# One scan per four state-space groups, with a coefficient tile that holds zeros, in place of four scans

## The chip, the core and the metric

The kernel runs on one core of one Trainium2 chip. The metric is the device time of one execution in microseconds (us), the median of several runs. TensorE (PE) multiplies matrices and loads its weights in parallel (PEld), VectorE (DVE), ScalarE (ACT) and GpSimd (POOL) work on tiles elementwise, and SyncE (SP), ACT and POOL issue DMAs. Each engine takes its instructions strictly in program order and waits at the first one whose inputs are not ready.

## The reference

One decoder layer over 512 tokens of width 1024. What matters here is the middle of it, the mixer:

```python
h = h + 0.5 * swiglu(rmsnorm(h), ...)             # first feed-forward half
z = rmsnorm(h) @ w_in                             # q, three k/v pairs, gates, u
o_nsa = nsa_attention(q, ..., gates)              # compressed, selected and windowed attention
o_s5  = s5_mixer(u, ...)                          # 32 groups of 16 channels, 64 complex states each
h = h + concat([o_nsa, o_s5]) @ w_out
h = h + 0.5 * swiglu(rmsnorm(h), ...)             # second feed-forward half, then a gated embedding
# s5_mixer, per group: x[t] = a * x[t-1] + b u[t],  y[t] = Re(c x[t]) + d u[t]
```

## The kernel before, in words

The feed-forward halves take the time from 0 to about 370 us and from about 650 us to the end; the mixer lies between. The activations are held transposed, weights come in units of 128x1024 through ACT's DMA queue, and each unit is split into two parts, `hi` (ACT, line 164) and `lo` (DVE, line 166), so that three matmuls with those parts give one product close to float32.

The state-space part ("S5") handles 512 tokens as 64 chunks of 8 tokens. `s5_in(j)` runs for j = 0 to 7, each for GC = 4 of the 32 groups: four small matmuls give `w` in the PSUM bank `ps_C`, four DVE operations turn it by a rotation that makes the decay real (`t1`, lines 982 to 985), a scan along the 64 chunks follows with one real coefficient per partition and group (`r8`), and one operation turns the result back into `z`. `s5_out(j)` multiplies `z`, the input `u8` and the constants `so` into the bank `ps_D`; ACT copies the outcome into `ysb` (line 1012) and then makes the constants `so` for the next j by two copies (`swapped`, line 998). After every second j, `s5_back` transposes `ysb` back into `yt`.

Around it the mixer does the projections (24 matmuls into `ps_A` each) and their rotary turn: `rotary` forms `r` and `rb` from two projections and the tables in `turn`, and sends the outcome through DRAM by SP's queue: `kd` for the keys, which come back as `kf` and are cast into `KA` (ACT) and `KB` (DVE); `qd` for the queries, which come back as `qf` and are cast into `QA` and `QB` (ACT lines 1261 and 1262, DVE line 1263). The compressed keys take the way `ra`, `kcd`, `cst`, `cs`, and the compressed values `ra`, `vcd`, `cst`, and then the space of `turn`. The score groups of a query block (three matmuls: `KA`, `KB` and the mask, into `ps_B` or `ps_C`, two buffers each) are followed by a row maximum on DVE (`nmax`, line 1284) and an exponential on ACT (line 916) that frees the buffer.

The order of the mixer's steps is given by a table of step names (`PLAN`). That is the order in which the program is written; the order on each engine is then made by a scheduler, which lets an instruction pass others when it expects, from its own estimate of durations, that its inputs are ready sooner. So another duration at one place changes the order of others around it. The two feed-forward halves and all steps from the values of query block 2 on have the same order in both kernels.

Of the kernel before, what the change touches and what calls it, by code (L numbers as in the profile page):

```python
# [10 lines left out]
F32 = mybir.dt.float32  # L11
# [4 lines left out]
OP = mybir.AluOpType  # L16
# [14 lines left out]
GC = 4  # L31
# [45 lines left out]
def block_kernel(ctx: ExitStack, tc: tile.TileContext, a: dict, out: bass.AP):  # L77
    nc = tc.nc
    V, S, G, PE = nc.vector, nc.scalar, nc.gpsimd, nc.tensor
# [12 lines left out]
    def bank(tag, shape=(128, 512), dt=F32):  # L92
        return psum.tile(list(shape), dt, tag=tag, name="ps_" + tag)
# [38 lines left out]
    def mm(o, lhsT, rhs, start, stop, **kw):  # L132
        return PE.matmul(o, lhsT, rhs, start=start, stop=stop, **kw)  # L133
# [417 lines left out]
    r8 = pers.tile([128, NG], F32, name="r8")  # L551
# [295 lines left out]
    def mixer(ctx):  # L847
# [31 lines left out]
        s5w = s5x.enter_context(tc.tile_pool(name="s5w", bufs=2, reuse_waits="tile"))  # L879
# [88 lines left out]
        zs = [s5w.tile([128, 2, GC, 64], F32, name="z", bufs=1, tag=f"z{i}") for i in range(2)]  # L968
        for z in zs:
            G.memset(z[:, :, :, 0:1], 0.0)  # L970

        def s5_in(j):
            si_ = s5w.tile([128, GC, 256], F32, tag="si", name="si", bufs=3)
            G.dma_start(si_, s5i[:, GC * j:GC * j + GC])
            so = s5w.tile([128, GC, 384], F32, tag="so", name="so")
            G.dma_start(so[:, :, 0:256], s5o[:, GC * j:GC * j + GC])
            co, si = si_[:, :, 128:192], si_[:, :, 192:256]
            w = bank(TW, (128, GC, 64))
            for g in range(GC):
                mm(w[:, g], si_[:, g, 0:128], u8[:, GC * j + g], True, True)  # L980
            t1, t2 = (s5w.tile([128, GC, 64], F32, tag=n, name=n, bufs=1) for n in ("t1", "t2"))
            V.tensor_tensor(t1, w, co, OP.mult)
            V.tensor_tensor(t2[64:128], w[0:64], si[0:64], OP.mult)
            V.tensor_tensor(t2[0:64], w[64:128], si[64:128], OP.mult)
            V.tensor_tensor(t1, t1, t2, OP.subtract)
            vv = s5w.tile([128, GC, 64], F32, tag="vv", name="vv", bufs=1)
            for g in range(GC):
                V.tensor_tensor_scan(vv[:, g], r8[:, GC * j + g:GC * j + g + 1].to_broadcast([128, 64]), t1[:, g],  # L988
                                     0.0, OP.mult, OP.add)
            z = zs[j % 2]  # L990
            cs_ = si_.rearrange("p g (a c) -> p a g c", c=64)[:, 2:4, :, 0:63]
            V.tensor_tensor(z[:, :, :, 1:64], vv[:, None, :, 0:63].to_broadcast([128, 2, GC, 63]), cs_, OP.mult)
            return so, z
# [34 lines left out]
        def s5_all():  # L1028
            pend = s5_in(0)
            swapped(pend[0], nm.scaled)  # L1030
            yield
            for j in range(NCH):
                nxt = s5_in(j + 1) if j + 1 < NCH else None
                yield
                if j % 2 == 0:
                    ysb = s5w.tile([64, 8, 128], F32, tag="ysb", name="ysb", bufs=1)
                last = s5_out(j, ysb, *pend)
                if nxt:
                    swapped(nxt[0], last)
                if j % 2:  # L1040
                    s5_back(j // 2, ysb)
                pend = nxt
                yield
# [379 lines left out]
    with ExitStack() as mctx:  # L1423
        out_half = mixer(mctx)
# [357 lines left out]
```

## Time and profile before

| | |
|---|---|
| median of 3 runs | 1042.17 us (1041.87 to 1045.31) |
| the profiled execution | 1042.74 us, its span 1041.0 us |
| PE busy | 1027.3 us (99% of the span) |
| DVE busy | 823.0 us (79%) |
| ACT busy | 506.2 us (49%) |
| POOL busy | 161.4 us (16%) |

Times in the trace count from the start of the span. A row of the timeline gives start and duration in us, the engine, the line of the program, the operation, output and inputs, the shape, how many instructions were merged, and in brackets how long the engine sat idle before it and what released it. Matmuls overlap: their listed durations are longer than the distance from one start to the next, so the distance of starts tells the pace.

### The profile page before, as it was taken

To read this page: it belongs to the slowest core of one execution; us is meant where nothing else is said; L and a number is where in the kernel's file an instruction comes from. 1 tells how busy PE (TensorE), PEld (TensorE's weight loads), DVE (VectorE), ACT (ScalarE), POOL (GpSimd) and SP (SyncE) were. 2 spreads that over 40 slices of the span, in tenths; PEclk is the share of its full clock that TensorE was granted. 3 is DMA by queue.
4 is the path that set the end of the run, shared out by engine and by line. 5 is a ranking of instruction groups with operands and counts; after the bars stand their busy time and mean duration, and the time that the engine had idled before them with its cause. 6 is when DMAs were issued, how large, how long until landed. Compare 5 with 4: busy or idle time off the path is not lost.

```text
span 1041.0 us, 15686 instructions
## 1 busy us (share of the span) xinstructions
PE 1027.3 (99%) x6048; PEld 875.4 (84%) x6049; DVE 823.0 (79%) x1382; ACT 506.2 (49%) x872; POOL 161.4 (16%) x181
## 2 busy tenths in 40 slices
PE   9999999999999999999999999999999999999997
PEld 6888888889989888777586688998999899899886
DVE  6799468988989766996789887996598588687676
ACT  6322232535326542667768855663365245255452
POOL 0003948207870200100000000000000000000001
PEclk9999999999999999999999999999999999999999
DMA  7424325736344739566510023433323333333412
GB/s 253 157 84 134 101 82 165 240 122 128 122 129 149 234 113 225 174 208 177 167 41 21 21 69 128 128 103 121 95 91 119 101 102 101 101 103 104 146 54 82
DMA packets 50618, 129.98 MB, mean 125 GB/s; under 512 B 10608, under 2 KB 17424, under 8 KB 50544
## 3 DMA queue, kind: packets, MB, share of 16 engines
q10 hardware_dynamic: 26352, 90.77, 27.7%
q0 software_dynamic: 6592, 18.48, 6.9%
q1 hardware_dynamic: 17600, 19.73, 6.2%
q8 instruction: 47, 0.77, 0.3%
q14 instruction: 27, 0.22, 0.1%
HBM read 112.81 MB, written 15.73 MB: 123 GB/s over the span
## 4 chain that ended last, share of the span: by engine, by line
PE 85%; DVE 6%; POOL 3%; issue 2%; DMA 2%; ACT 2%; SPq 0%; DVEq 0%; ACTq 0%; POOLq 0%
PE ps_A L133 25%; PE ps_C L133 25%; PE ps_B L133 20%; PE ps_D L133 15%; POOL ft L721 1%; POOL bt L720 1%; DVE lo L166 1%; DMA raw<-in_wpack 1%; DMA kd<-r 1%; DVE vv L988 0%; DMA h<-in_xT 0%; POOL ft L719 0%; DVE s L342 0%; POOL seen L559 0%; PE ps_D L727 0%
## 5 line engine op out<-in xcount | busy, mean ns | idle before, releaser
L164 ACT CAST hi<-raw 128x1024 fp32r<-128x1024 f32 (+2 forms) x143 | 144.4, 1010 | 248.9 <-PE ps_C L133 97.2
L133 PE MATMUL ps_C<-hq,hi 128*128 128x512 f32 x704 | 217.4, 390 | 0.2
L166 DVE TENSOR_TENSOR lo<-raw,hi 128x1024 fp32r<-128x1024 f32 (+2 forms) x143 | 173.4, 1213 | 42.9 <-ACT hi L164 42.1
L133 PEld LDWEIGHTS ps_C<-hq,hi 128*128 128x128 f32 x704 | 130.8, 188 | 28.0 <-DVE h L526 1.3
L133 PE MATMUL ps_C<-hq,lo 128*128 128x512 f32 x352 | 136.9, 389 | 0.0
L133 PE MATMUL ps_A<-xh,hi 128*128 128x512 f32 (+1 forms) x352 | 124.2, 353 | 0.4 <-ACT hi L164 0.4
L133 PE MATMUL ps_A<-xl,hi 128*128 128x512 f32 (+1 forms) x352 | 124.1, 352 | 0.3 <-DVE xl L192 0.3
L133 PE MATMUL ps_A<-xh,lo 128*128 128x512 f32 (+1 forms) x352 | 122.6, 352 | 0.5 <-DVE lo L166 0.5
L164 ACT CAST hi<-s 128x1024 fp32r<-128x1024 f32 x56 | 59.0, 1053 | 107.0 <-PE ps_D L133 63.6
L166 DVE TENSOR_TENSOR lo<-s,hi 128x1024 fp32r<-128x1024 f32 x56 | 70.6, 1262 | 20.2 <-ACT hi L164 20.0
L133 PEld LDWEIGHTS ps_C<-hq,lo 128*128 128x128 f32 x352 | 66.1, 188 | 13.9
L133 PEld LDWEIGHTS ps_A<-xh,hi 128*128 128x128 f32 x352 | 66.4, 189 | 10.5 <-ACT hi L164 0.7
L133 PEld LDWEIGHTS ps_A<-xh,lo 128*128 128x128 f32 x352 | 66.5, 189 | 9.8 <-DVE lo L166 1.1
L133 PEld LDWEIGHTS ps_A<-xl,hi 128*128 128x128 f32 x352 | 66.5, 189 | 9.8 <-DVE xl L192 0.8
L526 DVE SCALAR_TENSOR_TENSOR h<-ps_C,h 128x512 f32<-128x512 f32 x64 | 43.9, 686 | 36.6 <-PE ps_C L133 36.4
L133 PE MATMUL ps_B<-sh,lo 128*128 128x256 f32 x224 | 63.1, 282 | 0.3 <-DVE lo L166 0.3
L133 PE MATMUL ps_D<-sl,hi 128*128 128x256 f32 x224 | 63.1, 282 | 0.0
L133 PE MATMUL ps_B<-sh,hi 128*128 128x256 f32 x224 | 63.0, 281 | 0.0
L133 PE MATMUL ps_B<-sl,hi 128*128 128x256 f32 x224 | 62.9, 281 | 0.0
L133 PE MATMUL ps_D<-sh,hi 128*128 128x256 f32 x224 | 62.8, 280 | 0.0
L133 PE MATMUL ps_B<-xh,hi 128*128 128x512 f32 (+1 forms) x168 | 62.8, 374 | 0.0
L133 PE MATMUL ps_D<-sh,lo 128*128 128x256 f32 x224 | 62.6, 280 | 0.0
(435 smaller groups left out, 2473.2 us busy)
## 6 DMA issues: line engine op xcount, KB each, us to landing
raw<-in_wpack ACTq DMA_DIRECT2D x168, 512.0 KB, 3.6
si<-s5i POOLq DMA_DIRECT2D x8, 512.0 KB, 5.5
so<-s5o POOLq DMA_DIRECT2D x8, 512.0 KB, 5.7
h<-in_xT SPq DMA_DIRECT2D x8, 256.0 KB, 4.3
s5i<-fs POOLq DMA_DIRECT2D x1, 2048.0 KB, 11.4
xraw<-in_xT SPq DMA_DIRECT2D x8, 256.0 KB, 3.4
s5o<-gt POOLq DMA_DIRECT2D x1, 2048.0 KB, 13.3
s5i<-tcs POOLq DMA_DIRECT2D x2, 1024.0 KB, 10.5
```

What stands on the lines that cost most here:

```text
L133: return PE.matmul(o, lhsT, rhs, start=start, stop=stop, **kw)
L164: p, q = S.copy(hi[:, c], raw[:, c]), None
L166: q = V.tensor_tensor(lo[:, c], raw[:, c], hi[:, c].bitcast(F32), OP.subtract)
L526: V.scalar_tensor_tensor(h[:, m, :], o[m], 0.5, h[:, m, :], OP.mult, OP.add)
L720: G.tensor_tensor(bt, b2[:, 1], bc(psn[:, e]), OP.mult)
L721: G.tensor_tensor(ft[:, :, s_, :], ft[:, :, s_, :], bt, OP.add)
```

## The change

A tile `decay` (128 partitions, 4 groups, 64 chunks) gets a zero at the first chunk of each group once, by POOL. In each `s5_in(j)` ACT copies the four coefficients of each partition into the other 63 places of each group, and DVE runs one scan over all 256 places. The zero makes the state start anew at each group. The tile is single, so the copy for j waits for the scan of j-1, and the scan of j waits for the copy. The result `vv` now takes the space of `t2`; both are used by DVE alone.

```diff
+        decay = s5w.tile([128, GC, 64], F32, name="decay", bufs=1)
+        G.memset(decay[:, :, 0:1], 0.0)
...
-            vv = s5w.tile([128, GC, 64], F32, tag="vv", name="vv", bufs=1)
-            for g in range(GC):
-                V.tensor_tensor_scan(vv[:, g], r8[:, GC * j + g:GC * j + g + 1].to_broadcast([128, 64]), t1[:, g],
-                                     0.0, OP.mult, OP.add)
+            S.copy(decay[:, :, 1:64], r8[:, GC * j:GC * j + GC, None].to_broadcast([128, GC, 63]))
+            vv = s5w.tile([128, GC, 64], F32, tag="t2", name="vv", bufs=1)
+            V.tensor_tensor_scan(vv.rearrange("p g c -> p (g c)"), decay.rearrange("p g c -> p (g c)"),
+                                 t1.rearrange("p g c -> p (g c)"), 0.0, OP.mult, OP.add)
```

Lines behind the change stand two further down in the new kernel. The scheduler's order changes on every engine inside the mixer. Three places of it follow. A number behind a name tells buffers apart.

The first place is DVE at the first pair of query projections (`r_4033` and `rb_4034` before, `r_4031` and `rb_4032` now), while the keys are under way through DRAM. Before:

```order
L1055 TENSOR_TENSOR r_3935<-r_3935,rb_3936 128x512
L1056 TENSOR_TENSOR r_3937<-r_3937,r_3938 128x512
L166 TENSOR_TENSOR lo<-raw,hi 128x1024
L1051 TENSOR_TENSOR r_4033<-ps_A,turn 128x512
L1052 TENSOR_TENSOR r_4035<-ps_A,turn 128x512
L1053 TENSOR_TENSOR rb_4034<-ps_A,turn 128x512
L1054 TENSOR_TENSOR r_4036<-ps_A,turn 128x512
L1072 TENSOR_TENSOR KB<-kf,KA 64x512
```

All four products of the queries with the tables stood ahead of the first `KB`, which needs the keys back from DRAM. The same stretch of DVE in the new kernel:

```order
L1057 TENSOR_TENSOR r_3933<-r_3933,rb_3934 128x512
L166 TENSOR_TENSOR lo<-raw,hi 128x1024
L1058 TENSOR_TENSOR r_3935<-r_3935,r_3936 128x512
L1053 TENSOR_TENSOR r_4031<-ps_A,turn 128x512
L166 TENSOR_TENSOR lo<-raw,hi 128x1024
L1054 TENSOR_TENSOR r_4033<-ps_A,turn 128x512
L1074 TENSOR_TENSOR KB<-kf,KA 64x512
L1055 TENSOR_TENSOR rb_4032<-ps_A,turn 128x512
L1056 TENSOR_TENSOR r_4034<-ps_A,turn 128x512
```

Two of the four products now stand behind the first `KB`.

The second place is where the second pair of queries comes back from DRAM as `qf`. ACT before, from the split of a unit of 840 columns on:

```order
L164 CAST hi<-raw 128x840
L1023 COPY yt<-ps_D 128x512
L916 ACTIVATE gt<-yt 128x512
L1261 ACTIVATE QA<-qf 64x512
L1262 ACTIVATE QB<-qf 64x512
L1012 COPY ysb<-ps_D 64x2x8x16
L916 ACTIVATE ps_B,den<-ps_B,nmax 128x512
L1012 COPY ysb<-ps_D 64x2x8x16
L998 COPY so<-so 64x4x128 x2
```

Here the copies `yt` and `gt` were done while `qf` was awaited. ACT in the new kernel:

```order
L988 COPY decay<-r_121 128x4x63
L164 CAST hi<-raw 128x840
L1263 ACTIVATE QA<-qf 64x512
L1264 ACTIVATE QB<-qf 64x512
L1025 COPY yt<-ps_D 128x512
L916 ACTIVATE gt<-yt 128x512
L1014 COPY ysb<-ps_D 64x2x8x16 x2
L1000 COPY so<-so 64x4x128 x2
```

`yt` and `gt` moved behind the two casts that need `qf`, and ahead of `ysb` and `so`. DVE at the same place, before:

```order
L1284 TENSOR_REDUCE nmax<-ps_B 128x1
L166 TENSOR_TENSOR lo<-raw,hi 128x840
L1084 TENSOR_TENSOR ra<-ra,rb_4347 64x512
L1085 TENSOR_TENSOR ra<-ra,rb_4347 64x512
L922 SCALAR_TENSOR_TENSOR gt<-gt,yt 128x512
L1263 SCALAR_TENSOR_TENSOR QA<-qf,QA 64x512
```

The compressed keys `ra` were finished ahead of the operation that needs `qf`. DVE in the new kernel:

```order
L166 TENSOR_TENSOR lo<-raw,hi 128x840
L1286 TENSOR_REDUCE nmax<-ps_B 128x1
L1265 SCALAR_TENSOR_TENSOR QA<-qf,QA 64x512
L1086 TENSOR_TENSOR ra<-ra,rb_4337 64x512
L1087 TENSOR_TENSOR ra<-ra,rb_4337 64x512
L922 SCALAR_TENSOR_TENSOR gt<-gt,yt 128x512
```

The operation on `qf` moved ahead of both `ra`.

The third place is DVE where the compressed values come back (`cst`) and are put into the space of `turn`. Before:

```order
L1284 TENSOR_REDUCE nmax<-ps_C 128x1
L1263 SCALAR_TENSOR_TENSOR QA<-qf,QA 64x512
L1284 TENSOR_REDUCE nmax<-ps_B 128x1 x2
L1131 TENSOR_TENSOR turn<-cst,pe 128x8x32 x2
L922 SCALAR_TENSOR_TENSOR gt<-gt,yt 128x512
L1131 TENSOR_TENSOR turn<-cst,pe 128x8x32 x2
```

Two row maxima of `ps_B` stood ahead of all four. In the new kernel:

```order
L1286 TENSOR_REDUCE nmax<-ps_C 128x1
L1133 TENSOR_TENSOR turn<-cst,pe 128x8x32 x2
L1286 TENSOR_REDUCE nmax<-ps_B 128x1
L1133 TENSOR_TENSOR turn<-cst,pe 128x8x32 x2
L922 SCALAR_TENSOR_TENSOR gt<-gt,yt 128x512
L1286 TENSOR_REDUCE nmax<-ps_B 128x1
```

Both maxima moved behind operations on `cst`. On PE the groups of `s5_out` moved among the projections too: those of j = 2, 3 and 5 (counted from 0) come 4, 2 and 6 matmuls of `ps_A` earlier than before, and six more value matmuls (128x280) stand ahead of the eighth score group of `ps_B`.

## Prediction

> **What bounds the kernel now.** I read the head of the page first, then the busy times by stretches of the mixer.
>
> ```profile
> span 1041.0 us, 15686 instructions
> PE 1027.3 (99%) x6048; PEld 875.4 (84%) x6049; DVE 823.0 (79%) x1382; ACT 506.2 (49%) x872; POOL 161.4 (16%) x181
> ...
> 400.00:420.00 20.00, 20.00 (x110) 16.45 (x109) 13.66 (x28) 5.07 (x8) 1.90 (x3) 1.00 0.84 229
> 420.00:440.00 20.00, 20.00 (x156) 15.94 (x156) 19.60 (x43) 14.15 (x24) 2.63 (x4) 1.00 0.56 179
> 440.00:460.00 20.00, 19.92 (x146) 15.60 (x143) 19.38 (x40) 13.79 (x29) 2.81 (x4) 1.00 0.71 218
> 460.00:480.00 20.00, 18.17 (x145) 15.04 (x145) 16.37 (x33) 15.38 (x36) 1.41 (x2) 0.91 0.62 146
> 480.00:500.00 20.00, 20.00 (x132) 12.82 (x131) 10.33 (x21) 12.98 (x30) 0.57 (x1) 1.00 0.68 237
> ```
>
> The columns after the width are the busy times of PE, PEld, DVE, ACT and POOL, then the granted clock. PE is the bound over the whole span: its matmuls stay the same, so only its gaps can be won or made. The stretch that holds the scans (400 to 466 us) has DVE at 97 to 98% from 420 to 460 us, with PE still fed, and only one gap of note behind it. The timeline of PE shows that gap:
>
> ```profile
> 463.02 0.39 PE L133 MATMUL ps_A<-hi,xl 128*128 128x280 f32 x1
> 465.24 0.50 PE L133 MATMUL ps_B<-KA,QA 128*128 128x512 f32 x1 [1.83 <-ACT ps_B L916]
> ...
> 466.47 0.43 PE L133 MATMUL ps_A<-hi,xl 128*128 128x280 f32 x1
> 466.70 0.43 PE L133 MATMUL ps_A<-hi,xh 128*128 128x280 f32 x1
> ...
> 470.02 0.29 PE L133 MATMUL ps_A<-hi,xh 128*128 128x280 f32 x1
> 470.15 0.29 PE L133 MATMUL ps_A<-lo,xh 128*128 128x280 f32 x1
> ...
> 465.30:469.30 4.00, 4.00 (x16) 3.19 (x17) 3.91 (x7) 3.90 (x10) 0.00 (x0) 0.57 0.85 218
> ```
>
> PE sat idle 1.83 us before the eighth score group in `ps_B`. Right behind it, the granted clock in a stretch of 4.0 us was 0.57, and the matmuls of 280 columns start 0.23 us apart instead of 0.13. At half clock for about 3.4 us (0.43 x 4.0 / 0.5) that cost another 1.7 us. So gap and slow stretch together are worth 3.5 us. What ended last there:
>
> ```profile
> 441.65 0.68 DVE L1056 TENSOR_TENSOR r<-r,r 128x512 f32<-128x512 f32 x1
> ...
> 442.36 0.32 SPq L1058 DMA_DIRECT2D qd<-r  x1
> 448.09 0.59 SPq L1250 DMA_DIRECT2D qf<-qd  x1
> 451.21 1.19 SPq L1087 DMA_DIRECT2D kcd<-ra  x2
> ...
> 456.82 1.78 SPq L1250 DMA_DIRECT2D qf<-qd  x2
> ...
> 450.79 0.63 ACT L1261 ACTIVATE QA<-qf 64x512 fp32r<-64x512 f32 x1 [3.13 <-DMA qf<-qd]
> ...
> 453.54 1.25 ACT L998 COPY so<-so 64x512 f32<-64x512 f32 x2
> ...
> 463.24 0.63 ACT L1261 ACTIVATE QA<-qf 64x512 fp32r<-64x512 f32 x1 [3.57 <-DMA qf<-qd]
> ...
> 464.41 0.66 ACT L916 ACTIVATE ps_B<-ps_B,nmax 128x512 f32<-128x512 f32 x1
> ```
>
> The exponential at 464.41 us frees the buffer for the eighth score group. It stood on ACT behind two casts of `qf` that waited for a DMA until 463.24. That DMA was issued behind the way of the compressed keys (`kcd`, `cst`), and that way starts when DVE has made `ra`. So a chain of DVE order and DRAM round trips sets the gap, and not the length of the scans alone.
>
> **The change, part by part.** First the scan.
>
> ```profile
> L988 DVE TENSOR_TENSOR_SCAN vv<-r,t x32: 260/266/293, 401.3 to 463.0; 128x64 f32<-128x64 f32 x32
> ...
> 400.85 0.42 DVE L985 TENSOR_TENSOR t<-t,t 128x256 f32<-128x256 f32 x1
> 401.31 0.84 DVE L988 TENSOR_TENSOR_SCAN vv<-r,t 128x64 f32<-128x64 f32 x4
> 402.18 0.68 DVE L992 TENSOR_TENSOR z<-vv,si 128x504 f32<-128x504 f32 x1
> ...
> L1012 ACT COPY ysb<-ps_D x16: 349/369/372, 411.7 to 474.4; 64x256 f32<-64x256 f32 x16
> ...
> 427.84 0.63 ACT L1261 ACTIVATE QA<-qf 64x512 fp32r<-64x512 f32 x1 [0.18 <-DMA qf<-qd]
> ...
> 434.00 0.63 ACT L916 ACTIVATE gt<-gt 128x512 f32<-128x512 f32 x1 [2.61 <-DVE gt L922]
> ```
>
> One scan lists 0.266 us, but four occupy only 0.84, since they overlap (0.19 us apart). A single pass over 256 places is not in the trace. The elementwise rows give 0.26 us more for 248 more places, so 1.04 ns each and 0.15 us fixed; a scan of 64 is then 0.115 us over its fixed part, or 1.8 ns a place, and 256 places take 0.61 us. The bounds are 0.47 us (0.266 plus 192 places at 1.04 ns) and 0.84 us (four times the pitch, no gain). I take 0.61, from the scans' own row. DVE is relieved of 0.23 us in each of eight steps, 1.8 us in all (0 to 3.0). [...]
>
> ACT gains eight copies of 252 places, 0.37 us each by the row of `ysb`: 3.0 us on an engine that has 6 us to spare in each 20 from 420 to 460 us. The first stands where ACT waits anyway. The others add a wait on DVE: a copy waits for the scan before it, and all behind it on ACT wait too. At j = 3 the copy and the second `so` (0.37 and 0.62) stand ahead of the first `QA`, which before started at 427.84, so it and `QB`, `yt` and `gt` behind it start about 1.0 us later; ACT sat idle 2.61 us soon after, at 434.00, and DVE takes up `QA` only later. I cost that at nothing; if the cover goes, it is that 1.0 us. The zeros cost POOL one memset, in front of loads needed 50 us later: nothing. `vv` in the space of `t2` adds no wait, as DVE runs both in order.
>
> Now the moved steps; here lies the rest of the sum. At the first place of the order DVE waits for the keys:
>
> ```profile
> 415.19 0.69 DVE L1051 TENSOR_TENSOR r<-ps_A,turn 128x512 f32<-128x512 f32 x1 [2.91 <-DMA kd<-r]
> ...
> 417.37 0.69 DVE L1053 TENSOR_TENSOR rb<-ps_A,turn 128x512 f32<-128x512 f32 x1 [0.89 <-PE ps_A L133]
> 417.98 0.68 DVE L1054 TENSOR_TENSOR r<-ps_A,turn 128x512 f32<-128x512 f32 x1
> ...
> 419.64 0.68 DVE L1072 TENSOR_TENSOR KB<-kf,KA 64x512 fp32r<-64x512 f32 x1 [0.98 <-ACT KA L1070]
> ```
>
> The products at 417.37 and 417.98 filled that wait. Behind `KB` they fall into the stretch where DVE is full: 1.2 us more work there (two starts 0.6 us apart). The `z` of j = 4 also moves ahead of the second query outcome, 0.6 us. Against that stand three scans (-0.7) and, by the shorter scans of j = 0 and 1, an earlier write of the keys (-0.3). So the outcome that before started at 441.65 comes 0.8 us later, and with it its write, the load of `qf` (its wait of 5.3 us from 442.7 to 448.09 is for that write) and ACT's `QA`: 451.6 us.
>
> The second place needs four rows more, two of ACT and two of PE:
>
> ```profile
> 446.41 0.59 ACT L1023 COPY yt<-ps_D 128x512 f32<-128x512 f32 x1
> 447.03 0.63 ACT L916 ACTIVATE gt<-yt 128x512 f32<-128x512 f32 x1
> ...
> 454.84 0.39 PE L133 MATMUL ps_A<-xh,lo 128*128 128x512 f32 x1
> 455.07 0.39 PE L133 MATMUL ps_A<-xh,hi 128*128 128x512 f32 x1
> 455.38 0.66 PE L133 MATMUL ps_D<-so,z 128*64 128x128 f32 x8
> ```
>
> `yt` and `gt` (0.59 + 0.63) now stand between `QB` and `ysb`. ACT then runs 451.6 + 1.25 (QA, QB) + 1.2 + 0.75 (`ysb`) + 1.25 (`so`) = 456.0. On PE, `s5_out(5)` waits for that `so`. It started at 455.38, 0.6 us after `so` was done (453.54 + 1.25), and now stands 6 matmuls earlier, 6 x 0.23 = 1.4 us, so PE arrives at 454.0 and finds `so` at 456.1: a new gap of 2.1 us. On DVE, the operation on `qf` now blocks `ra`: DVE goes on at 452.3 instead of having `ra` done at 451.2, so `kcd` leaves at 453.6, 2.4 us later. SP issues in order, so the `cst` loads, the second `qf`, and the exponential behind its casts move by 2.4 us too. The eighth score group starts at 465.24 + 2.4 = 467.65. Six more matmuls of 280 columns (0.77 us) are done before it, so the net loss is 1.6 us. Seen from PE's gaps: 2.1 new, the old one 1.35 instead of 1.83.
>
> At the third place the ninth and tenth maxima stand behind `cst` of the values, which comes at least 2.4 us later. Counted by the same rows, the exponential for the tenth group comes about 1.3 us after PE wants it. This is the least sure term; between 0 and 1.3 I take 0.8, since ACT's order there has exponentials of `ps_C` that may be ready or not. The slow stretch of 1.7 us I leave as it is: one before, one after. The rest of the mixer (to 600 us) has nearly no gaps to win, and its new order I cost at nothing.
>
> Sum: scan on PE's path 0, since the relief is spent inside the chain (it is in the 0.8), + 1.6 + 0.8 = +2.4 us. The profiled execution took 1042.74 us, 1.7 over its span and 0.6 over the median; the sum stands against it, and I apply the difference to the median: 1042.17 + 2.4 = 1044.6 us, 0.23% slower. About 0.3%, or 3.1 us, is what a measurement of this kernel can tell from no change.
>
> **Rivals.** *Both gaps turn into slow stretches.* The new gap of 2.1 us is longer than the one that was followed by half clock. If each is followed by one, 1.7 us come on top, and with the third place in full (1.3) the loss is 1.6 + 1.7 + 1.3 = 4.6 us: 1046.8. Against it: PE at half clock arrives later at the second gap and so shrinks it. [...]
>
> *The old gap closes: faster.* The price is 1.83 + 1.7 = 3.5 us, so 1038.7. Of the gap of 1.83 us, the six matmuls cover 0.77 anyway, so the chain would have to come 1.1 us earlier than before, not 2.4 later. The writes of the queries land like this (size, then the median us to landing):
>
> ```profile
> qd<-r SPq DMA_DIRECT2D x4, 256.0 KB, 2.4
> ```
>
> The second query write was slower here, with 5.3 us until `qf` could be issued; 2 us less would bring `QA` to 449.6, before DVE and ACT stand at it. For it: the DMA share is 0.71 there, and the order of transfers changes. Against it: the same transfers remain, and the write itself starts later.
>
> *The moves cancel.* The new gap at `s5_out(5)` is lost from the old one, and nothing is left at the third place: within 1 us of 1042.2. It holds if `kf` comes 1 us earlier than I think and the 0.8 falls away.
>
> **How the numbers follow.** My forecast (+2.4, between +1 and +4) has 0.42, the two slow stretches 0.24, the cancelling 0.20, and the closed gap 0.14. Faster by over 0.3% is most of the last case and none of the others: 0.12. Slower by over 0.3% is the second case, 0.24, and the upper third of the first, 0.14: 0.38. Within 0.3%: 0.50. The range reaches from the closed gap at half of its price (1042.2 - 1.8 = 1040.4) to the second case with the cover of the copies gone as well (1046.8 + 1.0 = 1047.8). The unknown price of the scan moves the chain by three steps of at most 0.23 us one way and 0.14 the other, 0.7 or 0.4 us, and lies within that.
>
> **What would show it.** Right: scans of 0.6 to 0.7 us in eight rows; DVE idle about 3.5 us before the first `KB` and about 2 us before `QA` near 450; a gap of PE before `ps_D<-so,z` near 454 and a shorter one before the eighth score group near 466; `kcd` near 453.6. Wrong: no gap at 454, `QA` near 449, or a granted clock of 1.00 in all stretches from 440 to 480; or gaps of PE beyond 500 us, where I expect none.

## The result and the profile after

| | before | after |
|---|---|---|
| median of 6 runs each | 1042.81 us (1041.64 to 1045.31) | 1049.41 us (1048.83 to 1051.53) |
| ratio | | 1.0069, 95% interval 1.0053 to 1.0086 |
| the profiled execution and its span | 1042.74 us, 1041.0 us | 1049.26 us, 1047.4 us |

The changed kernel is slower by 0.69%, about 7 us. I forecast 1044.6 us, with a range up to 1047.8. The head of the page and the busy times by stretch of the changed kernel (columns as in the prediction):

```profile
span 1047.4 us, 15676 instructions
PE 1028.8 (98%) x6048; PEld 876.1 (84%) x6049; DVE 822.2 (78%) x1358; ACT 508.9 (49%) x880; POOL 160.7 (15%) x182
...
420.00:440.00 20.00, 18.82 (x135) 14.73 (x133) 18.64 (x32) 14.32 (x25) 2.63 (x4) 1.00 0.50 157
440.00:460.00 20.00, 18.31 (x144) 14.28 (x145) 18.21 (x30) 12.78 (x27) 2.28 (x4) 1.00 0.64 207
460.00:480.00 20.00, 17.21 (x131) 13.96 (x129) 15.50 (x29) 13.11 (x29) 1.94 (x3) 0.91 0.59 159
480.00:500.00 20.00, 18.28 (x133) 12.89 (x133) 10.93 (x22) 14.27 (x34) 0.00 (x0) 1.00 0.65 184
```

From 420 to 500 us PE is busy for 72.6 of 80 us, before for 78.1: 5.5 of the 6.4 us by which the span grew. DVE is less busy from 420 to 480 us than before, not more: it waits too. PE's gaps in the timeline:

```profile
432.09 0.66 PE L133 MATMUL ps_D<-so,z 128*64 128x128 f32 x8 [0.54 <-DVE z L994]
439.99 0.66 PE L133 MATMUL ps_D<-so,z 128*64 128x128 f32 x8 [0.63 <-ACT so L1000]
443.50 0.50 PE L133 MATMUL ps_B<-KA,QA 128*128 128x512 f32 x1 [1.31 <-ACT ps_B L916]
457.71 0.66 PE L133 MATMUL ps_D<-so,z 128*64 128x128 f32 x8 [0.38 <-ACT so L1000]
470.68 0.50 PE L133 MATMUL ps_B<-KA,QA 128*128 128x512 f32 x1 [2.79 <-ACT ps_B L916]
480.46 0.36 PE L133 MATMUL ps_A<-hi,xh 128*128 128x280 f32 x1 [0.28 <-DVE gp L1115]
494.54 0.43 PE L133 MATMUL ps_A<-raw,cs 128*63 128x256 f32 x1 [1.43 <-DMA raw<-in_wpack]
```

Before there was one gap of 1.83 us in all this. Now there are seven, 7.4 us together. The changed operations themselves look harmless (duration in ns: least, median, most):

```profile
L990 DVE TENSOR_TENSOR_SCAN vv<-decay,t x8: 680/691/693, 401.6 to 467.7; 128x256 f32<-128x256 f32 x8
L988 ACT COPY decay<-r x8: 395/402/402, 344.5 to 460.8; 128x252 f32<-128x252 f32 x8
```

So the reader has to follow the chain of waits. On DVE, then on SP's queue, then on ACT:

```profile
420.28 0.68 DVE L1074 TENSOR_TENSOR KB<-kf,KA 64x512 fp32r<-64x512 f32 x1 [4.65 <-ACT KA L1072]
...
425.15 0.68 DVE L1058 TENSOR_TENSOR r<-r,r 128x512 f32<-128x512 f32 x1
...
433.27 0.68 DVE L1265 SCALAR_TENSOR_TENSOR QA<-qf,QA 64x512 fp32r<-64x512 f32 x1 [0.54 <-ACT QA L1263]
...
444.69 0.68 DVE L1058 TENSOR_TENSOR r<-r,r 128x512 f32<-128x512 f32 x1
...
454.00 0.69 DVE L1265 SCALAR_TENSOR_TENSOR QA<-qf,QA 64x512 fp32r<-64x512 f32 x1 [1.11 <-ACT QA L1263]
...
455.44 0.69 DVE L1087 TENSOR_TENSOR ra<-ra,rb 64x512 f32<-64x512 f32 x1
...
465.38 1.09 DVE L1133 TENSOR_TENSOR cs<-cst,pe 128x256 f32<-128x256 f32 x2 [2.69 <-DMA cst<-kcd]
...
469.08 0.68 DVE L1286 TENSOR_REDUCE nmax<-ps_B 128x1 f32<-128x512 f32 x1
```

```profile
429.55 0.62 SPq L1252 DMA_DIRECT2D qf<-qd  x1
...
450.69 0.58 SPq L1252 DMA_DIRECT2D qf<-qd  x1
455.44 1.20 SPq L1089 DMA_DIRECT2D kcd<-ra  x2
460.16 0.46 SPq L1125 DMA_DIRECT2D cst<-kcd  x1
```

```profile
432.61 0.63 ACT L1263 ACTIVATE QA<-qf 64x512 fp32r<-64x512 f32 x1 [2.53 <-DMA qf<-qd]
...
453.34 0.63 ACT L1263 ACTIVATE QA<-qf 64x512 fp32r<-64x512 f32 x1 [3.63 <-DMA qf<-qd]
...
469.85 0.66 ACT L916 ACTIVATE ps_B<-ps_B,nmax 128x512 f32<-128x512 f32 x1 [1.98 <-DVE nmax L1286]
```

Four rows of before that the prediction does not show:

```profile
422.16 0.69 DVE L1056 TENSOR_TENSOR r<-r,r 128x512 f32<-128x512 f32 x1
...
425.13 0.62 SPq L1250 DMA_DIRECT2D qf<-qd  x1
...
454.33 0.46 SPq L1123 DMA_DIRECT2D cst<-kcd  x1
...
459.33 1.12 DVE L1131 TENSOR_TENSOR cs<-cst,pe 128x256 f32<-128x256 f32 x2
```

Read against the rows of before: the first query outcome (`L1058`, then `L1056` at 422.16) comes 3.0 us later, its `qf` is loaded 4.4 us later (then 425.13), the first `QA` runs 4.8 us later (427.84), and DVE now waits for it. The second outcome is 3.0 us late (441.65), its `QA` 2.6 (450.79). Behind that `QA` stands `ra`, so `kcd` leaves 4.2 us late (451.21). Its write took 4.7 us until `cst` could be loaded, against 3.1 before (451.21 to 454.33), so `cst` is 5.8 us late, and `cs` on DVE 6.0 (459.33). The row maximum behind `cs` waits with it, then the exponential, and PE stands 2.79 us. So 3.0 us at the first outcome have become 6.0 at `cs`. About 0.3 us of each of these delays is older than all this: the first scan starts at 401.6 us, before at 401.3. The rest of the way has three steps that add to the delay. The first query write took longer (from the start of its second half at 425.86 to the load 3.7 us, before 2.25 from 422.88), `ra` stood behind the wait for `QA` (4.2 us late at `kcd` against 2.6 at `QA`), and the write of `kcd` took 1.6 us longer. Half clock follows that gap as before (the stretch behind it):

```profile
470.70:474.70 4.00, 4.00 (x17) 3.63 (x18) 3.47 (x6) 3.92 (x9) 0.00 (x0) 0.57 0.76 203
```

### The profile page after: what moved, and what is told of

It reads as the page before. It is cut to its first block, busy times and chain, and to the rows that moved or that the text cites. A ratio compares the mean times of both kernels' runs of the same rounds, so it can differ in the third digit from the quotient of the medians.

```text
span 1047.4 us, 15676 instructions
## 1 busy us (share of the span) xinstructions
PE 1028.8 (98%) x6048; PEld 876.1 (84%) x6049; DVE 822.2 (78%) x1358; ACT 508.9 (49%) x880; POOL 160.7 (15%) x182
## 4 chain that ended last, share of the span: by engine, by line
PE 83%; DVE 5%; DMA 4%; POOL 3%; ACT 3%; issue 2%; SPq 0%; DVEq 0%; ACTq 0%; POOLq 0%
PE ps_C L133 24%; PE ps_A L133 23%; PE ps_B L133 20%; PE ps_D L133 15%; POOL ft L721 1%; POOL bt L720 1%; DVE lo L166 1%; DMA qf<-qd 1%; DMA raw<-in_wpack 1%; DMA qd<-r 0%; DMA h<-in_xT 0%; DMA kd<-r 0%; DMA kf<-kd 0%; POOL ft L719 0%; DVE s L342 0%
```

## The experiments

To part the arithmetic from the order, the instructions of the mixer are tied, engine by engine, into a given order by edges that set the order of issue and add no wait:

```diff
+for engine, places in ORDER.items():          # places in the order of tracing
+    for a, b in zip(places, places[1:]):
+        tc.add_manual_dep(kept[engine][b], kept[engine][a].name, nosync, reason="order")
```

Below, the fences show which rows move. The kernel before ran beside each, and all ratios are to it; its median moved between 1041.57 and 1042.81 us, so compare the ratios of two rows rather than their times.

| kernel | median us (least to most, runs) | ratio, 95% interval |
|---|---|---|
| changed | 1049.41 (1048.83 to 1051.53, 6) | 1.0069 (1.0053 to 1.0086) |
| four scans, new order | 1049.47 (1048.95 to 1050.86, 6) | 1.0067 (1.0049 to 1.0085) |
| one scan, old order | 1044.35 (1039.68 to 1047.20, 12) | 1.0007 (0.9988 to 1.0025) |
| changed, first place as before | 1048.53 (1047.35 to 1049.78, 6) | 1.0055 (1.0038 to 1.0072) |
| changed, `ra` first | 1046.18 (1045.32 to 1047.99, 7) | 1.0039 (1.0025 to 1.0054) |
| changed, `ra` and maxima as before | 1045.52 (1044.48 to 1045.87, 5) | 1.0035 (1.0023 to 1.0047) |
| changed, second place as before | 1045.29 (1043.29 to 1048.38, 12) | 1.0027 (1.0014 to 1.0041) |
| changed, DVE as before to 458 us | 1043.81 (1042.49 to 1047.77, 12) | 1.0025 (1.0016 to 1.0034) |
| one scan, old order up to 460 us | 1043.27 (1041.50 to 1046.21, 12) | 1.0011 (0.9999 to 1.0023) |
| one scan, old order, maxima early | 1041.59 (1040.20 to 1044.48, 12) | 0.9995 (0.9984 to 1.0007) |
| four scans, old order, maxima early | 1040.62 (1039.56 to 1044.77, 12) | 0.9988 (0.9974 to 1.0002) |
| four scans, the same and `KB` behind | 1040.69 (1038.90 to 1042.32, 11) | 0.9982 (0.9968 to 0.9996) |
| one scan, the same and `KB` behind | 1040.23 (1038.86 to 1041.64, 12) | 0.9980 (0.9970 to 0.9990) |

### Order or arithmetic

One scan with the old order:

```diff
 ORDER = every engine's order of the kernel before
+the scan of j where the four scans of j stood
+each copy into decay where ACT sat idle before
```

> One scan and the eight copies as in the changed kernel, but every engine's order in the mixer tied to that of the kernel before (each scan where the four stood, each copy where ACT sat idle before). If the loss of 6.6 us comes from the order alone: 1042 us, between 1040.5 and 1043.5, with PE gaps as before (one of about 1.8 us before the eighth score group near 465 us, half clock behind it). If the copies and the longer single scan make the loss: 1048 to 1050, with gaps before the matmuls that need z.

Four scans with the new order:

```diff
 ORDER = every engine's order of the changed kernel
-S.copy(decay...), one scan
+the four scans of j where the one scan of j stood
```

> Four scans without copies, as in the kernel before, but every engine's order in the mixer tied to that of the changed kernel. If the order makes the loss: 1049 us, between 1047.5 and 1050.5, with gaps near 432, 440, 443.5 and 470 us. If the copies and the single scan make it: 1042 to 1043.

The first gives 1.0007, the second 1.0067: the loss goes with the order and not with the scan or the copies (the interval of the first leaves room for at most 2.6 us of theirs). The gaps of the second stand where the changed kernel's do:

```profile
443.25 0.50 PE L133 MATMUL ps_B<-KA,QA 128*128 128x512 f32 x1 [1.43 <-ACT ps_B L916]
...
471.30 0.79 PE L133 MATMUL ps_B<-KA,QA 128*128 128x512 f32 x1 [3.32 <-ACT ps_B L916]
...
470.00:474.00 4.00, 2.70 (x10) 2.18 (x11) 3.94 (x7) 3.46 (x8) 0.00 (x0) 0.60 0.62 193
474.00:478.00 4.00, 4.00 (x18) 3.48 (x18) 2.46 (x5) 3.94 (x10) 0.00 (x0) 0.54 0.86 232
```

The old order with one scan has runs from 1039.7 to 1047.2 us, the kernel before beside it from 1040.1 to 1048.9. Its profiled execution is one of the shortest (1039.73), and it shows something that I had not looked for: the gap of 1.83 us is absent, though the order is the old one. Of its PE waits from 400 to 600 us, its second pair of `qf` (SP's queue) and the cast of it on ACT:

```profile
PE ps_C L133 <- DMA si<-s5i: 0.8, 1, 0.8
...
456.69 1.26 SPq L1252 DMA_DIRECT2D qf<-qd  x2
...
460.29 0.63 ACT L1263 ACTIVATE QA<-qf 64x512 fp32r<-64x512 f32 x1
```

The cast ran 3.6 us after the issue of the load, in the profile of before 6.4 us after it (456.82 to 463.24). So in these two executions, the only ones of the whole old order with a profile, the gap comes and goes with the landing of one load. That this makes the spread of the runs is likely, but not shown.

### Which move

The first place as before, on DVE alone:

```diff
 L1054 TENSOR_TENSOR r<-ps_A,turn
+L1055 TENSOR_TENSOR rb<-ps_A,turn
+L1056 TENSOR_TENSOR r<-ps_A,turn
 L1074 TENSOR_TENSOR KB<-kf,KA
-L1055 TENSOR_TENSOR rb<-ps_A,turn
-L1056 TENSOR_TENSOR r<-ps_A,turn
...
+L1058 TENSOR_TENSOR r<-r,r
 L166 TENSOR_TENSOR lo<-raw,hi
-L1058 TENSOR_TENSOR r<-r,r
```

The fence shows the rows of the queries. Two splits `lo` and a scan take their old places among the rows around them too.

> The changed kernel with its own order, except DVE around the first pair of queries (406 to 430 us), which gets the order of the kernel before: all four products ahead of the first KB, the query outcome ahead of the split of a unit. If the loss starts at this place (the first query outcome 3 us late, its qf 4.4 us late): qf is issued near 426 instead of 429.55, the gaps at 432, 440 and 443.5 us (2.5 us together) go, and part of the later ones: 1045, between 1044 and 1047. If it starts at the second place: 1048.5 to 1049.5.

The ratio falls to 1.0055 only, which the intervals do not part from 1.0069. The load of `qf` did go out earlier, but little of it arrived:

```profile
426.91 0.62 SPq L1252 DMA_DIRECT2D qf<-qd  x1
...
454.98 1.19 SPq L1089 DMA_DIRECT2D kcd<-ra  x2
...
430.77 0.63 ACT L1263 ACTIVATE QA<-qf 64x512 fp32r<-64x512 f32 x1
...
470.79 0.80 PE L133 MATMUL ps_B<-KA,QA 128*128 128x512 f32 x1 [3.36 <-ACT ps_B L916]
```

2.6 us at the issue became 1.8 at `QA`, 0.7 at DVE's operation on `qf` (432.61 against 433.27) and at the second outcome (444.01 against 444.69), and 0.5 at `kcd`. The gap at 440 us went; those at 432, 443 and 471 us stayed. My theory that all the loss starts here fell. Two things may hide a part of what the place is worth: this execution is the longest of the six, and the keys came later in it (the first `KB` at 421.43, in the changed kernel at 420.28).

The second place as before, on three engines:

```diff
 DVE
+L1086, L1087 TENSOR_TENSOR ra<-ra,rb
+L922 SCALAR_TENSOR_TENSOR gt<-gt,yt
 L1265 SCALAR_TENSOR_TENSOR QA<-qf,QA
-L1086, L1087 TENSOR_TENSOR ra<-ra,rb
-L922 SCALAR_TENSOR_TENSOR gt<-gt,yt
 ACT
+L1025 COPY yt<-ps_D, L916 ACTIVATE gt<-yt
 L1263, L1264 ACTIVATE QA, QB<-qf
-L1025 COPY yt<-ps_D, L916 ACTIVATE gt<-yt
 PE: s5_out(5) six matmuls later
```

> The changed kernel with its own order, except around the second pair of queries (451 to 458 us): DVE makes ra ahead of the operation on qf, ACT does yt and gt ahead of the casts of qf, and PE's s5_out(5) stands six matmuls later, all as before. If this place makes the gap near 470 us: kcd leaves near 453 instead of 455.4, the gap of 2.8 us shrinks by about 2, and the time is 1047, between 1046 and 1048. If the loss comes from the late first query: 1048.5 to 1049.5, because qf of the second pair is late anyway.

1.0027: this gives back about 4 us, more than either theory said. To see which part, the DVE rows of that fence alone:

> The changed kernel with its own order, except that DVE makes ra (two operations) ahead of the operation on qf; ACT and PE stay. If this alone is what undoing the second place gave back (4.1 us): kcd leaves near 453.6 instead of 455.4, the gap near 470.7 us shrinks by 1.8, and the time is 1045 to 1047.5. If it was the place of yt and gt on ACT or of s5_out(5) on PE: 1048.5 to 1049.5.

1.0039, about 3 of the 4 us (its interval and that of 1.0069 just touch). Its `kcd` on SP's queue, PE's gap before the eighth score group, and the stretch behind that gap:

```profile
452.76 1.20 SPq L1089 DMA_DIRECT2D kcd<-ra  x2
...
468.46 0.50 PE L133 MATMUL ps_B<-KA,QA 128*128 128x512 f32 x1 [1.54 <-ACT ps_B L916]
...
470.00:474.00 4.00, 4.00 (x40) 3.55 (x40) 2.45 (x4) 3.91 (x10) 0.00 (x0) 1.00 0.88 258
```

`kcd` leaves 2.7 us earlier than in the changed kernel (0.75 of that stands already at the gap near 443 us, 442.75 against 443.50, where the order is the same), the gap shrinks by 1.25 us, and no half clock follows. Its write was shorter too: `cst` is loaded 3.45 us later, at 456.21, in the changed kernel 4.72 us later. By the ratios, two operations of DVE that stood behind a wait were nearly half of the loss. What `yt` and `gt` on ACT and `s5_out(5)` on PE add (1.0039 to 1.0027) is within the intervals.

`ra` first, and the maxima of the first scores ahead of the second query outcome:

```diff
-L994 TENSOR_TENSOR z<-vv,si
 L1055, L1056 TENSOR_TENSOR rb, r<-ps_A,turn
+L1286 TENSOR_REDUCE nmax<-ps_B
...
-L1286 TENSOR_REDUCE nmax<-ps_B
 L1058 TENSOR_TENSOR r<-r,r
+L994 TENSOR_TENSOR z<-vv,si
```

> The changed kernel with two places of DVE as before: ra ahead of the operation on qf, and (439 to 445 us) the row maxima of the first scores ahead of the second query outcome, z of j = 4 behind it; the first place stays. If the gap of 1.3 us at 443.5 us came from these maxima, it goes, and the time is 1.3 below the run with ra alone: 1044 to 1045.5. If it came from the late first qf: no change, 1045.5 to 1047.

1.0035, not to be told from `ra` alone, and the gap at 442 us stayed, though the maximum was done by 440.8. The rows say who held it now:

```profile
440.12 0.67 DVE L1286 TENSOR_REDUCE nmax<-ps_B 128x1 f32<-128x512 f32 x1
...
440.29 0.40 ACT L988 COPY decay<-r 128x252 f32<-128x252 f32 x1 [1.40 <-DVE vv L990]
440.60 0.89 ACT L164 CAST hi<-raw 128x840 fp32r<-128x840 f32 x1
441.51 0.66 ACT L916 ACTIVATE ps_B<-ps_B,nmax 128x512 f32<-128x512 f32 x1
...
442.34 0.50 PE L133 MATMUL ps_B<-KA,QA 128*128 128x512 f32 x1 [1.20 <-ACT ps_B L916]
```

ACT sat 1.40 us at the copy into `decay`, which waits for the scan before it, and the exponential stood behind. By these rows the copy is a cost here, in a place where another wait had hidden it. No run shows what makes the gap at 443.5 us of the changed kernel: neither the first place alone nor these maxima take it away, and with all of DVE's order as before (next) 0.79 us of it are left.

All of DVE's order as before from 406 to 458 us (the three pieces above together):

> The changed kernel with DVE's order of the kernel before from 406 to 458 us (the query products, the maxima and z of the second query pair, ra); ACT's and PE's order stay those of the changed kernel. If the loss is DVE's order: 1043 to 1045, like the kernel with the old order on all engines up to 460 us (1043.3). If ACT's and PE's own moves (yt and gt behind the casts of qf, s5_out six matmuls earlier) cost something: 1045.5 to 1047, with a gap before the matmuls of so and z near 455 us.

1.0025: about 4.4 of the 6.9 thousandths. The old order on DVE, ACT and PE up to 460 us, the new one behind:

> One scan and copies; up to about 460 us the order of the kernel before on DVE, ACT and PE, from there to the end of the mixer the order of the changed kernel. If the loss is made before 460 us: 1042 to 1044.5. If the order behind 460 us has a part in it (maxima behind the wait for cst, loads issued later): 1045 to 1048.

1.0011 (0.9999 to 1.0023): most of the loss is made before 460 us. What the order behind it adds, with the old order ahead, is at most those 2.4 us.

### A version that beats both

The gap of the old order needs an exponential that stands behind casts that wait for `qf`. Two maxima (done in `ps_B` by 458.7 us) and their exponentials can go ahead of what waits for DRAM:

```diff
 DVE
+L1286 TENSOR_REDUCE nmax<-ps_B x2
 L1133 TENSOR_TENSOR cs<-cst,pe
...
-L1286 TENSOR_REDUCE nmax<-ps_B x2
 ACT
+L916 ACTIVATE ps_B<-ps_B,nmax x2
 L1263, L1264 ACTIVATE QA, QB<-qf
-L916 ACTIVATE ps_B<-ps_B,nmax x2
```

With one scan:

> One scan and copies in the order of the kernel before, with one more edit: the two row maxima of the score groups that were done in ps_B by 458.7 us go ahead of the cs operations on DVE, and their two exponentials go ahead of the casts of qf on ACT. If the gap of 1.8 us before the eighth score group and the half clock behind it (3.5 us together) come from exponentials that stand behind the wait for qf, they cannot occur any more: 1039.5, between 1038.5 and 1041, with a narrow spread of the runs. If the buffer is late for another reason, or the maxima moved ahead delay cs: no change against the first run of the old order, 1042.5 to 1044.5.

With four scans:

> The kernel before (four scans, no copies) in its own order, with the same edit of maxima and exponentials. If the scan's form costs nothing at an equal order, the same time as with one scan: 1039.5, between 1038.5 and 1041. If the single scan relieves DVE where it counts, it is 0.5 to 1.5 us slower than with one scan; if the copies disturb, faster than that.

0.9995 and 0.9988. Neither profile has a gap from 442 to 484 us or half clock there, though no ratio is clear of 1. The longest runs are 1044.5 and 1044.8 us, of the kernel before beside them 1045.4, so a smaller spread is not shown yet. The medians stay above the 1039.5 that I expected, since gaps of 0.4 to 1.1 us near 432 and 441 us stay. There DVE stands at `KB` until the keys land, with the query outcome behind it, so:

```diff
-L1074 TENSOR_TENSOR KB<-kf,KA
 L1057 TENSOR_TENSOR r<-r,rb
 ...
 L1058 TENSOR_TENSOR r<-r,r
+L1074 TENSOR_TENSOR KB<-kf,KA
```

With four scans:

> Four scans in the order of the kernel before with the maxima and exponentials early, and on DVE the first KB, which waits for the keys from DRAM, behind the first query outcome. If the gaps that runs of this order show near 432 and 441 us come from DVE standing at KB with the query outcome behind it: 1039 to 1040, 1 to 1.5 us below the same kernel with KB ahead. If they come from the casts on ACT or from the load of qf: no change, 1040 to 1041.5.

With one scan:

> The same with one scan and the copies: 1039 to 1040 if KB was the cause, 1040.5 to 1042 if not; equal to the kernel with four scans within 1 us if the form of the scan costs nothing at an equal order.

0.9982 (0.9968 to 0.9996) and 0.9980 (0.9970 to 0.9990): both beat the kernel before by 0.2%. That `KB` alone did the last step is not shown, as the intervals overlap with the pair without it. The traces speak for little: with one scan the second half of the first query write left 2.2 us earlier than without this move (421.15 against 423.33), but `qf` was loaded only 0.2 us earlier (425.37 against 425.55), since its load then waited 1.7 us for `KB`. The spread is smaller here: 23 runs from 1038.9 to 1042.3 us, the kernel before beside them from 1039.5 to 1046.5. PE's waits from 400 to 600 us with one scan, all of them:

```profile
PE ps_B L133 <- ACT ps_B L916: 0.4, 1, 0.4
PE ps_D L133 <- ACT so L1000: 0.3, 1, 0.3
PE ps_A L133 <- DMA raw<-in_wpack: 0.3, 1, 0.3
PE ps_D L133 <- ACT eh L916: 0.2, 1, 0.2
PE ps_D L133 <- DVE eh L1380: 0.2, 1, 0.2
```

One scan and four give the same time, within the intervals, at each of four orders: old, new, and these two.

## Why the prediction was wrong

- **The scan: nearly right, and worth nothing.** I took 0.61 us, it is 0.69; four overlapping scans took 0.84. The relief is 0.15 us in each of eight steps, 1.2 us, where I had 1.8. That the relief is not seen by PE is shown by the pairs at equal order.
- **The copies: right here, by luck of the neighbours.** 0.40 us each against my 0.37. ACT waited for a scan ahead of five of them, 6.5 us in all. That this cost no time rests on the pairs at equal order. My 1.0 us for the case that the cover goes was the length of a copy and of `so`; in the run with the maxima moved it was the wait for the scan instead, 1.40 us on ACT and 1.20 at PE, at another j than I named.
- **The late query outcomes: the step that failed.** I put the second outcome 0.8 us late, and 1.0 us at the first `QA` "at nothing". The moved work was as I said: the two products 1.2, `z` of j = 4 about 0.7. The rest was not. The earlier write of the keys should have given 0.3 us; `kf` was issued 0.55 earlier (414.98 against 415.53), but the first `KB` ran 0.64 later (420.28 against 419.64). The three scans should have given 0.7 and gave about 0.1. And the first `QA` was 4.8 us late (products, `KB`, 1.2 us for the split `lo` that now stands ahead of the first outcome, 1.4 for the longer write), so that DVE's operation on `qf` waited and cost 0.6. I had looked for slack behind `QA` on ACT and not at DVE. Together 3.0 us at the second outcome. In the run with the first place as before this is only 0.7 us less, but the keys came 1.15 us later in it, so how much of the 3.0 that place alone makes stays open.
- **The gaps ahead of 445 us: in no term.** I followed the late outcomes only to `s5_out(5)` and the eighth score group. Near 432, 440 and 443.5 us PE waited 2.5 us together, for `z` on DVE, for `so` and for an exponential on ACT. With the first place as before the one at 440 us goes; what makes the other two is not shown.
- **The second place: the way through `ra` and `kcd` right, its end and the sizes off.** `QA` at 453.34 instead of 451.6; `kcd` at 455.44 instead of 453.6; the eighth score group at 470.68 instead of 467.65. The 1.8 us missing in `kcd` are those of the second outcome. The write of `kcd` took 1.6 us longer, which I had left as it was. And what ended last was not the casts of `qf` on ACT, but the row maximum on DVE behind `cs`. I had carried over the releaser of before. The new gap at `s5_out(5)`, 2.1 us by my sum, is 0.38: PE itself was late by then.
- **The third place: not seen.** No gap stands at the ninth or tenth score group. The gap of 1.43 us at 494.5 us, for a weight unit, was in no term of mine. With four scans in the same order there is none (PE is busy all of 480 to 500 us), so the order alone does not make it.
- **Half clock: one stretch, as I had left it.** The rival in which both gaps turn slow did not come: the run went past its 1046.8 by gaps in other places. In the profile with `ra` first the slow stretch, 1.7 us by my sum, is gone (the clock is 1.00 from 460 to 480 us, in the changed kernel 0.91).
- **The rest of the mixer: right.** PE has no gap over 0.15 us from 500 to 600 us, and the order behind 460 us costs at most 2.4 us where the old order stands ahead of it.

The sum was +2.4 us, with 5.5 us of new gaps measured. The places that I had priced came to less than I said: 0.38 at `s5_out(5)`, 0.96 more at the eighth score group, nothing at the third place, 1.3 us together. The other 4.2 us are gaps that no term held. That the order decides was told rightly; where its delays reach PE was not.

## What to carry to other kernels

Where a scheduler makes the order, a change of a few operations is a change of the order, and the order can be worth more than the operations (here 1.0067 with the new order alone, 1.0007 with one scan alone): run the new arithmetic in the old order and the old in the new before judging either. When an order moves work behind an operation that waits for DRAM, follow the delay through every later round trip to the end, and ask at each who stands behind the waiting operation; two operations (`ra`) behind one wait were about 3 us here. And put work whose inputs lie ready ahead of work that waits for a transfer: the orders with the maxima early and `KB` behind were the fastest here (0.9980 and 0.9982), with a narrower spread than the kernel before (3.4 us in 23 runs against 7.0).

## What the runs showed of the hardware

Runs of one program (one scan, old order) spread over 7.5 us, from 1039.68 to 1047.20, and the cast behind the same pair of loads of `qf`, in the same order of issue, ran 3.6 us after their issue in its profile and 6.4 us in that of the kernel before. What decides their landing stays open; before, a load of constants (`so`, 512 KB, issued on POOL's queue at 457.45 us) is under way at the same time, with 144 packets beside the 818 of SP's queue from 456.8 to 463.3 us.

How long a write took went with its place in the order here. The first query write took 2.2 to 2.3 us, from the start of its second half to the load of `qf`, in the seven profiles where DVE makes this half ahead of the split `lo` (2.25 before), and 3.7 to 4.0 in the five where it comes behind (3.69 in the changed kernel; the two with `KB` behind are left out, as their load waits for `KB`). The write of `kcd` took 3.1 to 3.6 us in the ten profiles where it left by 452.9 us (3.12 before), and 4.6 to 5.0 in the four where it left at 454.7 or later (4.72 in the changed kernel). So a delay at the issue of a write was not passed on as it was, but grew by about 1.5 us. In eight of these nine late writes the load of a weight unit on ACT's queue had been issued 0.2 to 0.6 us ahead of the write, and in all the early ones 0.9 to 2.1 us behind it; no run moves that load alone, so the cause is not shown.

Half clock (a granted clock of 0.50 from 466 to 468 us before) came after some gaps only: after 1.54 us (`ra` first) the stretch behind ran at 1.00, after 1.83 (before) and 2.79 us (changed) the 4.0 us behind show 0.57, and after 3.32 us (four scans, new order) two stretches of 4.0 us show 0.60 and 0.54, about twice as long. So the gaps of 1.83 and 2.79 us each cost about 1.7 us more than their length (my estimate, 0.43 x 4.0 us), and the one of 3.32 us about twice that on top. What decides whether half clock follows a gap, and for how long, is not shown.
